# Softmax over rows of 512: sixteen-row blocks dealt out to partitions in another order

## The chip, the cores and the metric

The kernel runs on one core of one Trainium2 chip. The metric is device time in microseconds (us); lower is better. Before the change three runs took 159.81, 159.82 and 160.81 us, median 159.82 us. A profiled execution took 160.08 us, of which 158.8 us lie between its first and last instruction (its span). Names of engines as the profile has them: DVE is the vector engine, ACT the scalar engine, POOL the GpSimd engine, SP the engine that here only issues transfers, PE the matrix engine, which is unused. Sixteen DMA engines move data between DRAM and SBUF, the on-chip memory of 128 partitions; L145 is line 145 of the kernel.

## The reference

```python
def setup_inputs():
    batch, seq, dim = 16, 1024, 512
    return {
        "x": np.random.randn(batch, seq, dim).astype(np.float32),
    }

def reference(x: np.ndarray) -> np.ndarray:
    x_max = np.max(x, axis=-1, keepdims=True)
    exp_x = np.exp(x - x_max)
    return (exp_x / np.sum(exp_x, axis=-1, keepdims=True)).astype(np.float32)
```

That is 16384 independent rows of 512 float32 numbers, 33.55 MB in and 33.55 MB out.

## The kernel before

The rows are worked in 16 groups. A group is eight rows in each of the 128 partitions. Two groups make one load and one store: 16 consecutive rows per partition, which is one block of 32 KB that is contiguous in DRAM, 4096 KB for all partitions. There are eight loads L0 to L7 and eight stores S0 to S7 (the lists `LOADS` and `STORES`), each one instruction on SP's queue (L127 and L131).

Where a row lies is decided in one place, `in_dram`. It takes the 2048 rows of a load and cuts them so that partition p holds rows 16 p to 16 p + 15, its block p. Loads read through it and stores write through it, so a row goes back to where it came from, whatever the order. The tile in SBUF, `ring`, has room for 12 groups. `rows(g, n)` names the part of it that groups g to g + n - 1 use.

Each group passes three steps, in place. `rowmax` (L145, on DVE) takes the negated maximum of each row, for one group or, as `MM`, for the two of a load at once. `exps` (L134, on ACT) is a loop over the groups with eight instructions per group; each takes the exponential of one row with the negated maximum as its bias and leaves the row's sum. `scale` takes the reciprocals of the eight sums (L159, on DVE) and multiplies the rows by them (L161), on DVE for ten groups and on POOL for six. The order on DVE and POOL is written out by hand in `SEQUENCE`: M is a maximum, D a scaling on DVE, P one on POOL.

SP issues in the order written in `ORDER`, with the first six loads ahead of it, the very first even ahead of the start-up barrier:

```python
ORDER = """
S0 S1 L6 L7 S2 S3 S4 S5 S6 S7
"""
```

A store waits until both its groups are scaled (`store_scaled`). L6 waits until S0 has landed and L7 until S1 has, because they take over those places of the ring. Each load and each of the first two stores has a semaphore of its own; a transfer raises its semaphore by 16 when all of it has landed. All transfers share one queue, and each is divided among the 16 DMA engines.

## Time and profile before

| what | value |
|---|---|
| median of three runs | 159.82 us |
| the profiled execution | 160.08 us, span 158.8 us |
| DVE busy | 121.8 us (77% of the span), 36 instructions |
| ACT busy | 92.2 us (58%), 257 instructions |
| POOL busy | 42.3 us (27%), 10 instructions |
| DRAM traffic | 33.55 MB read, 33.55 MB written, 423 GB/s over the span |
| one load's issue on SP | 333 to 524 ns, median 404 |
| one store's issue on SP | 332 to 431 ns, median 338 |
| load, from issue to landing | 12.3 to 58.6 us |
| store, from issue to landing | 19.3 to 31.7 us |

How to read the page. It shows one execution. In the part with 40 slices each digit is the busy share of one fortieth of the span in tenths, 9 being 90% or more; for DMA it is the mean over the 16 engines, and the row below it has what they moved in GB/s. The chain of waits follows the end of the span back to what released each step. A row of the timeline has the start and the length in us, engine, line, operation, output and input, and in brackets how long the engine had been idle before it and what ended that.

### The profile page before, as it was taken

How to read it: one execution, taken by the hardware profiler on the slowest of the kernel's cores; microseconds unless marked ns; L12 is line 12 of the kernel's file. 1: busy time of each engine (PE TensorE's matmuls, PEld its weight loads, DVE VectorE, ACT ScalarE, POOL GpSimd, SP SyncE). 2: the span in 40 equal slices, each digit the busy share in tenths (PEclk: the TensorE clock that was granted, in tenths of full speed). 3: DMA queues.
4: the chain of work that ended last, by engine and by line, in shares of the span. 5: the costliest groups of instructions: out<-in, count | busy, mean ns of one | idle time of the engine just before them, and what ended most of it. 6: DMA issues, size and time to landing. Idle time of an engine off the chain costs nothing.

```text
span 158.8 us, 572 instructions
## 1 busy us (share of the span) xinstructions
DVE 121.8 (77%) x36; ACT 92.2 (58%) x257; POOL 42.3 (27%) x10
## 2 busy tenths in 40 slices
DVE  0008979999999999999999499999999999700000
ACT  0300699969406999999988990899599300000000
POOL 0000000000007903930970790079049300000000
DMA  7999999999999999999999999999999999999996
GB/s 264 438 479 405 405 495 421 396 438 471 413 405 438 471 405 396 396 413 471 438 396 462 446 413 405 454 421 438 438 421 446 413 446 438 438 421 438 429 429 264
DMA packets 2304, 67.11 MB, mean 423 GB/s; under 512 B 256, under 2 KB 256, under 8 KB 256
## 3 DMA queue, kind: packets, MB, share of 16 engines
q1 hardware_dynamic: 2304, 67.11, 98.9%
HBM read 33.55 MB, written 33.55 MB: 423 GB/s over the span
## 4 chain that ended last, share of the span: by engine, by line
DMA 45%; DVE 39%; issue 2%; DVEq 0%
DMA ring<-in_x_dram 26%; DVE ring L161 22%; DMA out_dram<-ring 20%; DVE stat L145 16%; DVE recip L159 1%; DVEq L144 0%
## 5 line engine op out<-in xcount | busy, mean ns | idle before, releaser
L134 ACT ACTIVATE ring<-ring,stat x128 | 90.4, 707 | 28.1 <-ACTq L151 28.1
L145 DVE TENSOR_REDUCE stat<-ring 128x16 f32<-128x8192 f32 (+1 forms) x10 | 69.5, 6956 | 15.7 <-DMA ring<-in_x_dram 15.7
L161 POOL TENSOR_TENSOR ring<-ring,recip 128x4096 f32<-128x4096 f32 x6 | 42.1, 7016 | 81.8 <-DVE recip L159 81.8
L161 DVE TENSOR_TENSOR ring<-ring,recip 128x4096 f32<-128x4096 f32 x10 | 51.1, 5109 | 0.3
L134 ACT ACTIVATION_READ_ACCUMULATOR ring<-ring,stat x128 | 23.8, 186 | 0.0
L181 ACT ACT_TABLE_LOAD x1 | 1.3, 1283 | 4.0 <-PEq L179 4.0
L159 DVE RECIPROCAL recip<-stat 128x8 f32<-128x8 f32 x16 | 3.0, 190 | 0.0
L215 POOL MEMSET const-float32-0.0<- 128x1 f32 x1 | 0.1, 98 | 0.2 <-issue 0.2
L215 POOL MEMSET const-bfloat16-1.0<- 128x1 bf16 x1 | 0.1, 102 | 0.0
L215 POOL MEMSET const-uint8-127<- 128x1 uint8 x1 | 0.1, 102 | 0.0
L215 POOL MEMSET const-float32-1.0<- 128x1 f32 x1 | 0.1, 98 | 0.0
## 6 DMA issues: line engine op xcount, KB each, us to landing
ring<-in_x_dram SPq DMA_DIRECT2D x8, 4096.0 KB, 25.9
out_dram<-ring SPq DMA_DIRECT2D x8, 4096.0 KB, 24.0
```

The source lines that it names most:

```text
L134: return nc.scalar.activation(out=row, in_=row, func=EXP, bias=one, scale=1.0, accum_out=one)
L145: nc.vector.reduce_max(out=cols(stat, g, groups), in_=rows(g, groups), axis=AX, negate=True).then_inc(maxima, groups)
L159: nc.vector.reciprocal(out=cols(recip, g), in_=cols(stat, g)).then_inc(inverted, 1)
L161: engine.tensor_mul(out=rows(g), in0=rows(g), in1=spread(cols(recip, g))).then_inc(scaled[store_of(g)], 1)
L181: nc.scalar.preload_act_table(EXP)
L215: nc = _bacc.Bacc("TRN2", target_bir_lowering=False, num_devices=1)
```

## The change

The 128 blocks of a load go to the partitions in another order. Before, partition p holds block p. After, partition 8 e + i holds block 16 i + e, for e from 0 to 15 and i from 0 to 7: partitions 0 to 7 hold blocks 0, 16, 32, ... 112, partitions 8 to 15 hold blocks 1, 17, ... 113. In the instruction the DRAM side's list of addresses becomes one of two levels, 16 entries 32 KB apart and under each eight entries 512 KB apart, with 32 KB per entry; the SBUF side still lists 128 partitions. Loads and stores change alike. `by_engine` returns what `rows` returns. The instructions of the compute engines, their order and all waits are the same as before.

```diff
+    def by_engine(g, n):
+        return rows(g, n)
+
...
         part = t[P * GROUP * LOAD_AT[k] : P * GROUP * (LOAD_AT[k] + LOADS[k]), :]
         first = (g - LOAD_AT[k]) * GROUP
-        part = part.rearrange("(p r) d -> p r d", p=P)
-        return part[:, first : first + groups * GROUP, :]
+
+        part = part.rearrange("(i e r) d -> e i r d", i=P // 16, e=16)
+        return part[:, :, first : first + groups * GROUP, :]
 
     def load(k):
         g, n = LOAD_AT[k], LOADS[k]
-        return nc.sync.dma_start(out=rows(g, n), in_=in_dram(x_rows, g, n))
+        return nc.sync.dma_start(out=by_engine(g, n), in_=in_dram(x_rows, g, n))
 
     def store(k):
         g, n = STORE_AT[k], STORES[k]
-        return nc.sync.dma_start(out=in_dram(out_rows, g, n), in_=rows(g, n))
+        return nc.sync.dma_start(out=in_dram(out_rows, g, n), in_=by_engine(g, n))
```

## The prediction

> **What bounds the kernel now.** I read the DMA part of the page first, because the slices show DMA at 9 tenths or more from the second slice to the last but one and no engine that steady.

> ```profile
> DMA  7999999999999999999999999999999999999996
> GB/s 264 438 479 405 405 495 421 396 438 471 413 405 438 471 405 396 396 413 471 438 396 462 446 413 405 454 421 438 438 421 446 413 446 438 438 421 438 429 429 264
> DMA packets 2304, 67.11 MB, mean 423 GB/s; under 512 B 256, under 2 KB 256, under 8 KB 256
> q1 hardware_dynamic: 2304, 67.11, 98.9%
> ```

> All traffic is on one queue, and its packets fill 98.9% of what sixteen DMA engines have in 158.8 us. Of 2304 packets 256 are tiny (one per engine and transfer, the completion), so 2048 carry data: 67.11 MB / 2048 is 32 KB, one partition's sixteen rows. Each of the sixteen transfers gives every engine eight such packets. Next, stretches of the span, split where loads end and stores begin (columns: stretch, length, busy time of DVE, ACT and POOL, clock, DMA share, GB/s):

> ```profile
> 4.00:57.00 53.00, 43.63 (x11) 32.18 (x88) 7.02 (x1) 1.00 1.01 435
> 102.00:157.00 55.00, 35.67 (x12) 20.51 (x58) 14.03 (x2) 1.00 1.00 433
> ```

> The first stretch is all loads, the second all stores: 435 and 433 GB/s, 27 GB/s for each engine, whichever way the data go and whatever the compute engines do. Third, the timeline of DVE gives the price of one transfer: the first two row maxima that wait for new loads start 9.68 us apart.

> ```profile
> 12.37 8.74 DVE L145 TENSOR_REDUCE stat<-ring 128x8 f32<-128x4096 f32 x2 [12.37 <-DMA ring<-in_x_dram]
> 22.05 4.42 DVE L145 TENSOR_REDUCE stat<-ring 128x8 f32<-128x4096 f32 x1 [0.94 <-DMA ring<-in_x_dram]
> ```

> So a packet takes 9.68 / 8 = 1.21 us, and 16 x 9.68 = 154.9 us of the 158.8 us span are transfers end to end. The other 3.9 us are the start (12.37 - 9.68 = 2.7) and 1.2 for the end and a few slow packets. Last, the issue rows and the chain of waits:

> ```profile
> ring<-in_x_dram SPq DMA_DIRECT2D x8, 4096.0 KB, 25.9
> out_dram<-ring SPq DMA_DIRECT2D x8, 4096.0 KB, 24.0
> DMA 45%; DVE 39%; issue 2%; DVEq 0%
> ```

> A transfer lands 24 to 26 us after its issue though it needs 9.68: one or two others stand ahead of it. The chain's 39% on DVE is the route by which the trace explains the last issue, not a stall of DMA; while DVE works, the queue is full. The kernel is DMA from end to end.

> **The change part by part.** No compute instruction is added, removed or moved; the softmax runs along a row, so it is the same work whichever row a partition holds, and DVE, ACT and POOL keep their times. The two row lists are rewritten in the same way for loads and stores, so each row returns to its place. Per partition it is still one run of 32 KB: still 2048 data packets. Three things differ.

> First, issuing. The DRAM side's list has two levels (16 x 8 blocks) and the SBUF side's one (128). The trace has no such issue. The nearest rows are the issues of before, 332 to 524 ns each; I bound the extra from 0 (or a gain of at most the first issue's 0.38 us) to 0.52 us each, and take 0.2. Fifteen of sixteen lie behind a queue with 20 us of work. SP issues nothing else, so what waits behind a longer issue is the next issue only. The first is on the path: +0.2 us.

> Second, DRAM addresses. At one instant the engines now read sixteen blocks next to one another and an engine's own eight lie 512 KB apart, where before the block of partition p + 1 followed that of p. The traffic reads and writes DRAM at 435 and 433 GB/s with different placements in time, so I see no DRAM limit at this rate and take nothing. The bounds: the lowest full slice of the page, 396 GB/s instead of 433, would add 16 x 9.68 x (433/396 - 1) = 14.5 us; the gain cannot exceed the 1.2 us of slow packets and end.

> Third, which engine carries which partitions, the large term. Sixteen outer entries over sixteen engines means that engine e carries one entry: partitions 8e to 8e + 7, in that order, as the change's own name has it. In the old form, 128 entries on both sides, nothing in the trace says which eight an engine had. All that is seen is that sixteen engines at once ran at 27 GB/s each, with equal speed in both directions, so the limit isn't the direction's or DRAM's but one per engine: either the engine's own pace, or its way into SBUF, with sixteen ways used by one engine each. If it is the way, a new division of partitions is safe only if it also gives each engine a way of its own at each moment. If two engines that step in lockstep through their eight partitions share a way, every packet takes 2 x 1.21 us. The bounds for a transfer are 9.68 (no meeting) and 19.36 (always in pairs); no row lies between. I take the upper end, less the lead that one engine of a pair has, because packets of neighbouring partitions follow one another in the same order on all engines, which makes a meeting last. The completions of the first load lie within 0.7 us, those of the last store within 1.1 us; two of sixteen in a spread of 0.9 us differ by a third of it, 0.3. A pair that meets on four packets, then on the next four, saves its lead twice a transfer: 19.36 - 0.6 = 18.76 us.

> [...]

> The sum: 16 x 18.76 = 300.2; 3.9 of start and end; 0.2 of issuing: span 304.3. The profiled execution took 160.08 us, 1.28 beyond its span, and the median of the runs is 0.26 below it: 304.3 + 1.28 - 0.26 = 305.3, say **305 us**. Behind that nothing else is late: L6 waits for the landing of S0 and L7 for that of S1, as now, but with the other transfer queued; load 7, the tenth transfer, would land near 2.7 + 10 x 18.76 = 190 us, and stores S2 to S5 then fill 75 us, while the last four groups need some 40 us (from the wait's end at 90.7 us to the last scaling's at 137.8 it is 47 now, beside other work).

> **The rivals.** (a) One direction alone meets, writes into SBUF or reads from it: 8 x 9.68 + 8 x 18.76 + 5.1 = 233 us. Against it: both run at one pace now. (b) Pairs meet at first and drift apart until one is four packets ahead; then no packet is shared. That costs four packets once: 159.8 + 0.2 + 4.84 = 165 us, more if it is slow. For it: the completions' spread grew from 0.7 to 1.1 us. Against: equal sharing keeps a lead as it is. (c) The DRAM side slows by the bound above: 174 us. [...] (d) The other side, not slower: the pace is the engine's own (a way into SBUF carries 54 GB/s or more), or the division over engines does not follow the list and the change does only the address part. Then 159.8 + 0.2 = 160 us. It decides wherever two engines on one way still finish a packet in 1.21 us. (e) Faster: only the 1.2 us of slow packets and end are there to win, 158.6 us. (f) Worse than doubled, three engines to a way or lost time at each switch: 16 x 3 x 9.68 + 5 = 470 us at most.

> **How the numbers follow.** Forecast 0.57, since a pace that is the same in both directions and for all engines speaks for a way per engine, and the list that set the division is just what is rewritten; (d) has what the engine's own pace would explain as well. Its own range 280 (a lead of 1.1 us: 16 x 17.16 + 5.1) to 318 (no lead, 315, plus 1%). Rivals: (a) 0.10, (b) 0.12, (c) 0.03, (d) 0.10, (e) 0.02, (f) 0.06. The range 164 to 318 takes in the forecast, (a), (b) and (c), 0.82. About 1% is what a measurement of this kernel tells from no change. Faster by over 1%: 0.02, generous to (e); within: 0.10, case (d); slower: the rest, 0.88.

> **What would show it.** The forecast is right if GB/s falls to about 217 in the all-load and the all-store stretch alike, the DMA share stays near 1, the first row maximum starts at 21 to 22 us instead of 12.37 and the second waiting one 19 us later. (a) shows 217 in one stretch and 430 in the other; (b) slow slices at the start and 430 behind them; (c) an even 400; (d) the old page. The forecast is wrong at its root if the load stretch still shows 435.

## The result and the profile after

The changed kernel takes 273.56 us (median of four runs, 270.68 to 280.1) against 159.88 us before: 1.704 times as long, 95% interval 1.694 to 1.714. The ratio leaves out the run of 280.1 us, which counts as a slow one. The profiled execution took 270.68 us with a span of 269.4 us.

The DMA part of the page of the changed kernel, in the order in which it was shown of the kernel before:

```profile
DMA  9999989989999998999999999999999999998520
GB/s 234 195 195 234 214 175 234 234 165 224 234 195 195 234 229 170 224 234 394 229 209 277 243 248 214 238 224 307 389 321 321 341 355 360 394 389 360 229 83 24
DMA packets 2304, 67.11 MB, mean 249 GB/s; under 512 B 256, under 2 KB 256, under 8 KB 256
q1 hardware_dynamic: 2304, 67.11, 94.0%
```

Packets and bytes are the same to the last one, and the engines are still counted busy for 94% of the span, but they move 249 GB/s instead of 423. Each packet is in flight for longer: 0.940 x 16 x 269.4 / 2048 is 1.98 us where before it was 0.989 x 16 x 158.8 / 2048, or 1.23 us. A busy share near 1 did not say here that a transfer ran at its best.

The stretches of the changed kernel (stretch, length, busy time of DVE, ACT and POOL, clock, DMA share, GB/s):

```profile
4.00:120.00 116.00, 62.02 (x18) 56.05 (x155) 18.71 (x3) 1.00 0.99 208
...
200.00:220.00 20.00, 19.90 (x8) 11.40 (x32) 7.02 (x1) 1.00 0.99 334
220.00:240.00 20.00, 5.26 (x3) 0.00 (x0) 0.00 (x0) 1.00 1.01 383
240.00:260.00 20.00, 0.00 (x0) 0.00 (x0) 0.00 (x0) 1.00 0.63 259
```

While only loads run, the pace is 208 GB/s, less than half of 435. In the stores of the end it climbs to 383 GB/s; then the engines finish one by one, and from 240 us on a part of them is idle. The timeline of DVE has the loads one by one:

```profile
22.23 8.74 DVE L149 TENSOR_REDUCE stat<-ring 128x8 f32<-128x4096 f32 x2 [22.23 <-DMA ring<-in_x_dram]
42.15 4.42 DVE L149 TENSOR_REDUCE stat<-ring 128x8 f32<-128x4096 f32 x1 [11.17 <-DMA ring<-in_x_dram]
...
121.66 8.69 DVE L149 TENSOR_REDUCE stat<-ring 128x16 f32<-128x8192 f32 x1 [6.42 <-DMA ring<-in_x_dram]
```

From the first load to the sixth it is (121.66 - 22.23) / 5 = 19.89 us per load, where it was 9.68. Issues to landing, and the chain of waits:

```profile
ring<-in_x_dram SPq DMA_DIRECT2D x8, 4096.0 KB, 50.5
out_dram<-ring SPq DMA_DIRECT2D x8, 4096.0 KB, 47.0
DMA 30%; DVE 27%; another core or an unknown queue 26%; SPq 0%; issue 0%; DVEq 0%
```

Both directions take about twice as long to land, 50.5 and 47.0 us where it was 25.9 and 24.0. Where 26% of the chain could not be attributed, the share of DMA is not to be read as having fallen. The compute engines' own times are what they were: DVE 122.4 us, ACT 92.5, POOL 42.3.

### The profile page after: what moved, and what is told of

It is laid out like the page before. It is cut to its first block, busy times and chain, and to the rows that moved or that the text cites. A ratio compares the mean times of both kernels' runs of the same rounds, so it can differ in the third digit from the quotient of the medians.

```text
span 269.4 us, 572 instructions
## 1 busy us (share of the span) xinstructions
DVE 122.4 (45%) x36; ACT 92.5 (34%) x257; POOL 42.3 (16%) x10
## 2 busy tenths in 40 slices
DMA packets 2304, 67.11 MB, mean 249 GB/s; under 512 B 256, under 2 KB 256, under 8 KB 256
## 3 DMA queue, kind: packets, MB, share of 16 engines
q1 hardware_dynamic: 2304, 67.11, 94.0%
## 4 chain that ended last, share of the span: by engine, by line
DMA 30%; DVE 27%; another core or an unknown queue 26%; SPq 0%; issue 0%; DVEq 0%
DMA ring<-in_x_dram 30%; DVE ring L165 14%; DVE stat L149 13%; DVE recip L163 0%; SPq L131 0%; SPq L135 0%; DVEq L148 0%
## 6 DMA issues: line engine op xcount, KB each, us to landing
ring<-in_x_dram SPq DMA_DIRECT2D x8, 4096.0 KB, 50.5
out_dram<-ring SPq DMA_DIRECT2D x8, 4096.0 KB, 47.0
```

## The experiments

Three causes were open: *shared ways* (an assumption: engine e now carries partitions 8e to 8e + 7, and two engines whose runs start 32 partitions apart use one way into SBUF), *addresses* (adjacent blocks of DRAM in use at one instant), and *list form* (a list of two levels is slow by itself). No view names the engine of a packet, so each run turns one of these alone.

### The same adjacency with 32 entries of four

```diff
-        part = part.rearrange("(i e r) d -> e i r d", i=P // 16, e=16)
+        part = part.rearrange("(i e r) d -> e i r d", i=4, e=32)
```

> The DRAM list of both directions becomes 32 entries of four (partition 4 c + j holds block 32 j + c) instead of 16 of eight; still two levels, still neighbouring blocks one entry apart, output unchanged. Theory (shared ways: engine e got the eight partitions 8e to 8e+7, and engines whose runs start 32 partitions apart meet on one way into SBUF): sixteen engines cannot take one entry each, fours of partitions go together as they may have done in the kernel before, and if an engine gets two fours that lie on one way of its own the time is that of before, 159 to 162 us, at 430 GB/s in loads and stores. Rival addresses (adjacent blocks in DRAM at one instant are slow): adjacency is kept, so 255 to 280 us. Rival list form (a list of two levels is slow by itself): 255 to 280 us. If the theory holds but the division hands engine e entries 2e and 2e+1, the eight partitions are those of the change and it is 270 us too; then this run tells nothing between them.

It took 160.75 us, 1.0054 times the kernel before (1.0040 to 1.0068). The timeline and the query for the loads (issue time in ns, least, median and most):

```profile
12.78 8.75 DVE L149 TENSOR_REDUCE stat<-ring 128x8 f32<-128x4096 f32 x2 [12.78 <-DMA ring<-in_x_dram]
22.47 4.42 DVE L149 TENSOR_REDUCE stat<-ring 128x8 f32<-128x4096 f32 x1 [0.94 <-DMA ring<-in_x_dram]
```

```profile
L131 SPq DMA_DIRECT2D ring<-in_x_dram x8: 571/596/666, 0.0 to 81.8; - x8
```

The loads are 9.69 us apart, as before. So neither a list of two levels nor adjacency in DRAM was slow by itself here; 16 entries of eight were, with loads 19.89 us apart. That the two lists give the engines different partitions is inferred from the pace. What is left is a start 0.41 us later (12.78 against 12.37) behind issues that take 596 ns instead of 404.

### The list of 16 entries with other addresses

```diff
-        part = t[P * GROUP * LOAD_AT[k] : P * GROUP * (LOAD_AT[k] + LOADS[k]), :]
...
-        part = part.rearrange("(i e r) d -> e i r d", i=P // 16, e=16)
-        return part[:, :, first : first + groups * GROUP, :]
+        part = t.rearrange("(i e k r) d -> k e i r d", i=8, e=16, k=8)
+        return part[k]
```

> The list stays 16 entries of eight, so the division of partitions over engines stays that of the change, but the blocks lie elsewhere: partition 8 e + i of transfer k holds block 128 i + 8 e + k of the whole input, so that engines read blocks 256 KB apart and no two adjacent ones at one instant; output unchanged. Shared ways: as the change, 260 to 285 us, the loads at 19.9 us each. Addresses: back towards 160 us, or at least some other pace than 19.9 us per load. List form: 260 to 285 us.

It took 274.42 us, with the loads as far apart as in the change:

```profile
22.75 8.74 DVE L146 TENSOR_REDUCE stat<-ring 128x8 f32<-128x4096 f32 x2 [22.75 <-DMA ring<-in_x_dram]
42.71 4.42 DVE L146 TENSOR_REDUCE stat<-ring 128x8 f32<-128x4096 f32 x1 [11.22 <-DMA ring<-in_x_dram]
```

19.96 us. Together the two runs clear the addresses: adjacent blocks with the other division are fast, 9.69 us per load, and blocks far apart with this division are slow, 19.96. The second run is the weaker half: an engine's own blocks lie 4 MB apart in it, and that this alone makes it slow is unlikely only because its loads keep the change's pace to 0.4%. The twins below use one set of addresses.

### The same lists on two places in SBUF

A kernel of six loads and six stores of 64 partitions, with lists of 16 entries of four; nothing is computed, and only the first 6144 rows of the output are written, with copies of the input. Its twin differs in one number:

```diff
-BASE = 0
+BASE = 32
...
        part = ring[BASE : BASE + HALF, k * 16 * d : (k + 1) * 16 * d]
```

> Six loads of 64 partitions (0 to 63) and, when all have landed, six stores of the same; no computation, the first 6144 rows of the output get a copy of the input's and the rest is left out. Lists of 16 entries of four, so sixteen engines carry four partitions each, four 32 KB packets per transfer: 4.84 us at full pace. Shared ways: engine e and engine e + 8 hold runs 32 partitions apart and meet on every packet, with no other way to drift to: 9.7 to 10 us per transfer, 210 to 220 GB/s in loads and stores alike, 60 us of loads and 60 of stores, 122 to 130 us in all. Addresses or list form: slow here as well as in the twin on partitions 32 to 95.

> The same six loads and stores with the same lists and the same DRAM addresses, on partitions 32 to 95. Shared ways: engines 0 to 7 hold partitions 32 to 63, engines 8 to 15 hold 64 to 95; if 64 and above lie on other ways than 32 to 63, no two engines meet and each transfer takes 4.84 us, 430 GB/s: 29 us of loads, 29 of stores, 62 to 70 us in all. [...] Addresses or list form: no difference between the twins, both 122 to 130 or both 62 to 70 us.

They took 128.64 and 65.93 us. A stretch of the loads and one of the stores, on partitions 0 to 63:

```profile
2.00:60.00 58.00, 0.00 (x0) 1.00 1.01 208
67.00:125.00 58.00, 0.00 (x0) 1.00 0.99 208
```

and on partitions 32 to 95 (the columns are POOL's busy time, clock, DMA share and GB/s):

```profile
2.00:30.00 28.00, 0.00 (x0) 1.00 0.98 412
36.00:62.00 26.00, 0.00 (x0) 1.00 1.03 444
```

### The change with its pairs put out of step

```diff
+            if k == 0:
+                for j in range(8):
+                    at_p, n = (32 + j, 12) if j < 4 else (76 + j, 4)
+                    extra = nc.sync.dma_start(
+                        out=ring[at_p : at_p + 4 * (n - 1) + 1 : 4, 10 * GROUP * d :],
+                        in_=x_rows[: n * 16, :].rearrange("(p r) d -> p (r d)", r=16),
+                    ).then_inc(early, 16)
...
```

The lines left out make L5 wait until the extra loads have landed.

> The change as it is, lists and addresses included, with eight small extra loads behind the first load (32 KB per partition into a part of the ring that L5 overwrites later; L5 waits for them): four that twelve engines carry and four that four engines carry, one packet per engine each, so that of every two engines whose runs start 32 partitions apart one falls four packets behind. Output unchanged. Shared ways: L0 lands after 20 us as in the change; behind the extra loads two such engines are never on the same four partitions' way, so the later loads land 9.7 to 11 us apart instead of 19.9. Time 160 + 10 (L0) + 10 (extra packets of the engines that carry both kinds) = 180 us, 170 to 215 if some pairs fall back into step. Addresses, or list form: nothing about them is changed, the loads stay at 19.9 us each and the time goes up to 280 to 290 us.

Four runs took 225.83 to 245.25 us, median 238.78: neither 180 nor 280. The stretches show why:

```profile
22.00:32.00 10.00, 8.75 (x2) 4.72 (x13) 0.00 (x0) 1.00 1.01 210
32.00:42.00 10.00, 0.00 (x0) 6.67 (x20) 0.00 (x0) 1.00 0.92 210
42.00:52.00 10.00, 0.00 (x0) 0.00 (x0) 0.00 (x0) 1.00 0.99 419
...
72.00:82.00 10.00, 10.00 (x3) 3.08 (x9) 3.23 (x1) 1.00 0.99 419
82.00:92.00 10.00, 9.96 (x5) 10.00 (x29) 3.79 (x1) 1.00 1.00 429
...
102.00:122.00 20.00, 16.36 (x6) 18.85 (x55) 10.54 (x2) 1.00 0.99 283
122.00:142.00 20.00, 8.60 (x1) 3.44 (x10) 3.49 (x1) 1.00 0.99 251
```

Behind the extra loads the same transfers run at 419 GB/s, and the completions of loads L2 to L5 come in three groups of engines 4.9 us apart, which is four packets at full pace (4 x 1.21). Nothing about lists, addresses or partitions has changed; only the moment at which the engines of a pair reach a partition has. That shows a meeting in time.

The order outlives the first store, S0, which completes in the same three groups (91.2 to 101.0 us) and lands 9.69 us after L5. It is lost at the second, S1. The timeline of DVE and that of SP (two issues, of which S1's is the second):

```profile
87.39 4.42 DVE L165 TENSOR_TENSOR ring<-ring,recip 128x4096 f32<-128x4096 f32 x1
```

```profile
70.01 22.39 SPq L135 DMA_DIRECT2D out_dram<-ring  x2
```

S1 could be issued only when this scaling had ended, at 91.8 us. The four leading engines had ended their last data packet of S0 at 90.7 us and started the next at 93.1, so half of their lead of 4.9 us went by in waiting; from there on packets take up to 2.55 us again, and the pace falls to 283 and 251 GB/s. The forecast of the total failed at this, and at the extra loads, which held the engines up for 20 us where 10 were forecast.

One thing the meeting of pairs does not explain. Each of the 128 data packets that start between 21.1 and 40.8 us takes 2.26 to 2.57 us, on all sixteen engines. By the theory only some engines meet there: the first four extra loads put the first eight engines on partitions 32 to 63, where no other engine is at that time. Either a pair that meets holds up the others while loads run, or the engines' shares are not quite what the theory has; no run here decides it.

### Each direction alone

The output's blocks stand in another order in both runs; each row's computation is the same.

```diff
+        if not apart:
+            return part.rearrange("(p r) d -> p r d", p=P)
         part = part.rearrange("(i e r) d -> e i r d", i=P // 16, e=16)
...
-        return nc.sync.dma_start(out=by_engine(g, n), in_=in_dram(x_rows, g, n))
+        return nc.sync.dma_start(out=by_engine(g, n), in_=in_dram(x_rows, g, n, True))
...
-        return nc.sync.dma_start(out=in_dram(out_rows, g, n), in_=by_engine(g, n))
+        return nc.sync.dma_start(out=in_dram(out_rows, g, n, False), in_=by_engine(g, n))
```

The run with new stores has True and False the other way round.

> Loads in the new form, stores in the old one (each store puts partition p's rows at block p, so the output's blocks stand in another order; the computation per row is the same). Shared ways: the loads keep 19.9 us each, 210 GB/s; the stores run at 9.7 us, 430 GB/s, once the loads are through: eight loads at 19.9, eight stores at 9.7 and 5 us make 242 us if loads L6 and L7, which run between stores, keep the pairs in step, less if they fall out of step there (230). Addresses or list form: the same split can come out, so the run mainly prices the two directions apart: rival (a) of the prediction has one direction at full pace in the change itself, which the trace of the change already denies.

> Loads in the old form, stores in the new one (output's blocks in another order, per row the same computation). Shared ways with reads from SBUF held up as much as writes into it: stores begin at 19.4 us each; in the change the eight stores and last two loads took about 148 us where 94 would be full pace, so stores drift apart somewhat: 8 x 9.7 + 8 x 14.8 + 5 = 201 us, 185 to 235. If reads from SBUF never meet, 160 to 165 us, and the slow stores of the change come from the state its loads leave behind.

New loads with old stores took 239.3 us: 79.4 us over before, or 9.9 us for each of eight loads. Old loads with new stores took 200.79 us: 40.9 us for eight stores, 5.1 each. The two add up to 120.3 us, near the change's 113.7. The stretches with new loads alone, first loads, then the old stores S0 and S1, then L6 and L7, then stores:

```profile
4.00:120.00 116.00, 62.03 (x18) 56.90 (x158) 19.54 (x3) 1.00 0.99 213
122.00:140.00 18.00, 11.93 (x4) 10.38 (x29) 5.96 (x1) 1.00 1.02 422
140.00:160.00 20.00, 0.18 (x1) 1.01 (x4) 1.06 (x1) 1.00 1.03 221
...
200.00:220.00 20.00, 13.31 (x5) 0.00 (x0) 0.00 (x0) 1.00 1.01 434
```

The pace switches with the form of the transfer, and stores of the old form leave the pairs in step: L6 and L7 are slow again, 221 and 236 GB/s, and the pace is back at 431 and 434 as soon as they are through.

### The stores alone, behind the loads

In part, against the twin on partitions 0 to 63:

```diff
-HALF = 64
+HALF = 128
...
-    for k in range(N):
-        nc.sync.dma_start(out=in_dram(out_rows, k), in_=here(k)).then_inc(stored, 16)
+    for k in range(STORES):
+        nc.sync.dma_start(out=in_dram(out_rows, k), in_=here(k % N)).then_inc(stored, 16)
```

> Six loads in the form and order of the change, on all 128 partitions; when all have landed, eight stores in the same form (the last two repeat the first two parts of the ring), issued one behind the other; no computation, so the output holds copies of input rows. It asks why the stores of the change ran faster than its loads. Theory that stores drift apart by themselves: loads at 19.9 us each, 119 us; stores start at 210 GB/s and rise towards 400 within the eight, 8 x 14.8 = 118 us or less, with the engines ending 20 to 40 us apart. Theory that the mixture of loads and stores in one queue pulls the pairs apart: with no load between them the stores stay at 19.4 to 19.9 us each, 208 to 216 GB/s to the end, 155 to 160 us for the eight, and the engines end within 1 or 2 us.

254.89 us; the stretches, of which the first is the loads and the others the stores:

```profile
4.00:119.00 115.00, 0.00 (x0) 1.00 1.01 210
125.00:145.00 20.00, 0.00 (x0) 1.00 0.97 211
145.00:165.00 20.00, 0.00 (x0) 1.00 1.02 256
...
185.00:205.00 20.00, 0.00 (x0) 1.00 1.01 293
205.00:225.00 20.00, 0.00 (x0) 1.00 0.99 333
```

With no load among them the stores begin at the loads' pace and get faster one after another. The engines' completions of the first store lie within 1.2 us (145.32 to 146.55), those of the second within 4.0, of the third within 6.4 and of the fourth within 8.6 (190.8 to 199.4). So stores leave their step by themselves, though the eight needed 129 us rather than the 118 expected. Why pairs that read from SBUF drift and pairs that write into it do not (the completions of each of the change's first six loads lie within 0.6 us) was not found; no run here looks at how a shared way is granted.

### The issue alone

```diff
+    nc.dge_precook = False
     nc.at_finalize(loads_at_the_head)
```

> The kernel before with its lists and addresses unchanged and the builder's prepared form of a transfer switched off, so that each issue on SP takes as long as an issue with a list of two levels. It prices the issue term alone, 0.2 us in the prediction, against the kernel of 32 x 4 lists, which was 0.8 us slower than before with new addresses as well. If the issue is all of that, the time is 160.5 to 160.8 us and the first row maximum starts at 12.7 to 12.8 us; if the addresses cost the rest, 159.9 to 160.3 us.

160.26 us, 1.0029 times before (1.0019 to 1.0040), with the first row maximum at 12.56 us:

```profile
L128 SPq DMA_DIRECT2D ring<-in_x_dram x8: 497/578/655, 0.0 to 81.5; - x8
```

So the longer issue is worth 160.26 - 159.88 = 0.38 us between medians. In the two traces the first issue takes 0.56 us instead of 0.38, and the first row maximum starts 0.19 us later; the other half of the 0.38 is not seen at the head. The 32 x 4 kernel was 160.75 - 159.93 = 0.82 us over the kernel before on its chip; the other 0.44 us are left for its somewhat longer issues and its addresses together. No version that does the whole work beat the kernel before.

## Why the prediction was right, and where it was off

**The bound** was read rightly: DMA from end to end, with no compute engine late. The sign and the cause followed from it, and the range held the time. That it did is luck in part: it reached down to 164 us for rivals (a) to (c), and none of them came as described.

**Issuing**, +0.2 us within 0 to 0.52: the issue alone measured 0.38 us between medians and 0.19 in the trace. **DRAM addresses**, nothing: the run with far blocks lies 0.9 us from the change, within the change's own scatter, the 32 x 4 lists leave 0.44 us at most, and out of step the change's own addresses gave loads 9.80 us apart (52.08 to 91.28 us for four) against 9.68; rival (c) falls as an account of the time, though a per cent is not excluded.

**Which engine carries which partitions**: the mechanism was right as far as the runs reach. The twins on partitions 0 to 63 and 32 to 95 show the shared ways apart from everything else, 128.64 against 65.93 us, and the run out of step shows that meeting on them in time is what costs, 210 GB/s against 419 with the same lists. That engine e carries partitions 8e to 8e + 7 stays inferred, and so does the step from pairs to all sixteen engines. The choice between the engine's own pace and its way into SBUF, which the trace of before could not make, falls to the way; rival (d) is out.

**The size of the term** is the step that was off: "two of sixteen in a spread of 0.9 us differ by a third of it, 0.3", hence 18.76 us for every transfer, and a forecast of 305 us whose own range, 280 to 318, missed 273.56. That a pair meets on four packets and then on the next four, and saves 0.6 us a transfer by it, was the author's estimate, and no run shows it; the run out of step showed that a step of four packets gives 419 GB/s, and no other step was tried. Two things stood in its place. Loads had no such saving and cost a little more than twice, 19.89 us, so the sixth landed at 121.6 us where 2.9 + 6 x 18.76 = 115.5 was forecast, 6.1 us more. And one price was used for both directions. From there to the end at 269.4, ten transfers took 147.8 us, 14.8 each including a ragged end, where 187.6 and 1.2 were forecast: 41 us less, although the end itself grew: the completions of the last store spread over 20.4 us (248.9 to 269.3) where they had spread over 1.1. The net, 41 - 6.1, is the miss in spans (304.3 - 269.4 = 34.9).

**The rivals**: (a), one direction alone, is denied, as both are slowed. (b), pairs that drift apart, is right of the stores in kind, though not in its price of 4.84 us once (the new stores alone cost 40.9), and wrong of the loads. The argument against it, that equal sharing keeps a lead as it is, holds for the loads alone: in the change they keep none (completions within 0.59 us at L0, 0.56 at L5), and in the run out of step they keep one of four packets.

**The signs to look for**: 208 GB/s in the load stretch (217 named), the first row maximum at 22.23 us (21 to 22 named), the next waiting one 19.92 us later (19 named). The store stretch did not stay at 217.

## What to carry to other kernels

The form of a transfer's address list, not only its bytes and its partitions, decided here how fast the DMA engines reached SBUF, by the account here through which engine touches which part of it: 16 x 8 against 128 cost a factor of two in the loads, 19.89 against 9.68 us, where 32 x 4 cost 0.5% of the time. When a transfer of long runs is slow while its busy share is near 1, compare the mean time of a packet (here 1.98 us) with that of a good stretch (1.21), and, if the tile has 64 partitions, move it by 32 (here from 128.64 to 65.93 us) before suspecting DRAM. A reordering for the sake of DRAM has to show that DRAM is the limit; equal paces for reads and writes, 435 and 433 GB/s, were a sign, though no proof, that it was not.

## What had not been expected

Loads that meet stayed in step for six transfers without a change of pace (208 GB/s), at 19.89 us rather than 19.36, twice 9.68, while stores that meet climbed from 211 to 333 GB/s within eight transfers. A lead of four packets between the engines of a pair gave full pace for four loads (419 GB/s) and one store (landed 9.69 us behind the last load) and was lost when the leading engines had to wait for an issue, from 90.7 to 93.1 us. The tile of 64 partitions ran at 412 and 444 GB/s when it started at partition 32, at 208 when it started at 0. And the extra transfers of one packet per engine completed 2.5 us apart, where a packet at full pace takes 1.21 us; the packets of L1 that other engines carried beside them took as long, so it is not a price of small transfers alone.
